# A two-layer hybrid trunk on one core: PSUM banks and norm weights of the SSD scan, row counts, sinks and rope of the sliding-window attention

## The chip, the core and the metric

The kernel runs on one core of a Trainium2 chip as one program. The core has TensorE (PE; its weight loads are shown as PEld), VectorE (DVE), ScalarE (ACT), GpSimd (POOL) and SyncE (SP, which here only issues DMAs). The metric is the device time of one execution in microseconds; lower is better. PSUM has eight banks of 512 f32 per partition, which is all that PE can write to.

## The reference

One token sequence of 1024 positions and width 1024 goes through two layers. Each layer projects the normalised input once and feeds three branches from it: sliding-window attention (SWA: 8 query heads, 2 key heads, rotary, one sink logit per head), forgetting attention (FoX) and a Mamba-2 SSD scan. Their outputs are concatenated and projected back; a memory cross-attention follows. Cut to the parts that the change touches:

```python
def rms_norm(x, w):
    return x * lax.rsqrt(jnp.mean(x * x, axis=-1, keepdims=True) + EPS) * w

def apply_rope(x, cos, sin):            # x1, x2: halves of the head
    return jnp.concatenate([x1 * c - x2 * s, x2 * c + x1 * s], axis=-1)

# sliding_window_attention, per block of 128 queries against 256 keys
scores = jnp.where(mask, q @ k.T * hd ** -0.5, NEG_INF)
m = jnp.maximum(jnp.max(scores, -1, keepdims=True), sink)
p = jnp.exp(scores - m)
probs = p / (jnp.sum(p, -1, keepdims=True) + jnp.exp(sink - m))

# ssd_chunked, per chunk of 128 positions and head h
y_diag = einsum('lsg,lsgh,sghp->lghp', c @ b.T, decay, xs)
y_off  = einsum('lgn,ghpn,lgh->lghp', c, carry, exp(acs))
yc = y_diag + y_off + d_skip * xs
yc = rms_norm(yc * silu(z), ssm_norm_w)
y  = concatenate([ya, yb, yc]) @ w_out
```

## The kernel before

Everything is f32 in effect. A large product is made of three fp32r matmuls: an operand is split into a high part (`hi`, an ACT copy, lines 75 to 79) and the remainder (`lo`, DVE or POOL, lines 81 to 85), and `mm3` (L110 to L113) adds high by high, low by high and high by low. Activations live transposed, features on the partitions, in two tiles `hhi` and `hlo` of 8 blocks of 128 features by 1024 positions.

**Order.** PE runs in the order in which the code emits its instructions. `mixer` weaves a main stream (FoX, then SWA, then the SSD scan) with a fill stream (projections, convolutions, gates, the output projection): the main stream yields what its step costs PE, or a point of a planned clock before which it does not go on, and `weave` puts fill work there (L297 to L325). The other engines' orders are made by a scheduler when the program is built. Each engine runs its list in order, so an instruction that waits holds up all that stand behind it. SP issues nearly all DMAs, in order.

**SWA.** There are 32 units per layer, 4 pairs of heads (t) by 8 query blocks (i), so 64 in all. `swa_project` (L740) makes Q of a pair by `roped` (L707): a projection into the PSUM tile `acc`, a scaled ACT copy to `qs`, four SBUF-to-SBUF DMAs that swap the halves, then cos on DVE (L719), sin on POOL (L720) and their sum (L721). A head's Q1 holds the high part twice, on partitions 0 to 63 and 64 to 127, K1 holds the high part of K above the low part of K, and Q2 holds Q's low part on 64 partitions. A unit's scores (`swa_scores`, L757) are two pairs of matmuls, one pair per head: Q1 by K1 over 128 rows (L769) and Q2 by K1's upper half over 64 rows (L770). Then DVE adds the mask and takes the maximum (L772), takes the smaller of the negated maximum and the negated sink (L778); L779 (DVE) and L780 (ACT) give exp(sink - m) in two columns, L782 (ACT) the exponentials with their row sums, L785 and L786 (DVE) the whole sum and its reciprocal, and POOL scales the tile Pt (L787). Three units later in the main stream `swa_turn` transposes Pt on PE (L798), ACT and DVE split it (ph, pl), and L830 multiplies by V. Pt rotates over four buffers under a tag that FoX uses too; the Q tiles rotate over three.

**SSD.** `ssd_scan` runs 16 units per layer, 8 chunks (c) by 2 groups (g). `before` of a unit is emitted one unit ahead: two matmuls `df` (L1069), C by B into the PSUM tile `pt` (`cb`, L1074), two activations that make the decay W (L1077, L1078), the mask (L1080), and W times `cb` (L1081). `after` makes the carried part in `yo` (L1095), the chunk state in `st` (L1105), the diagonal part in `yd` (L1124), adds them to Y (L1097, L1101, L1128), multiplies by the gate (L1129) and sums squares (L1130). `finish` of the chunk before follows each unit with g = 0: the root on POOL (L1142), the scaling of both halves Y on ACT (L1144), then for each half four transposes into `pt` (L1149) and, one block of 128 features after the other, `hi` (L79) and `lo` (L83) with a per-partition norm weight. `pt`, `yo`, `st` and `yd` are one PSUM bank each, `df` is two, and `acc` of the fill stream two.

## Time and profile before

| | us |
|---|---|
| median of 3 runs (2633.95 to 2640.07) | 2637.05 |
| the profiled execution, its own time | 2644.48 |
| its span, first to last instruction | 2642.7 |
| DVE busy in it | 1590.9 |
| ACT busy in it | 1219.2 |
| POOL busy in it | 1085.6 |

The spans of the stages of layer 0, by the first and last instructions of their lines: SWA from about 716 to 876 us, SSD from about 876 to 1110 us; of layer 1, SWA from about 1960 to 2107 us and SSD from about 2107 to 2350 us. The rest is the input norms, the projections, FoX and the cross-attention. In the rows of the profile `line engine op out<-in` comes first, then the count, the busy time, the mean of one in ns, and the idle time of the engine ahead of it with what ended that. A row of a timeline begins with its start and its duration in us; the durations of matmuls overlap, so it is the distance of two starts that tells what one costs. "L1149 <- DVE hlo L83" means that the instruction of line 1149 could start when that of line 83 was done.

### The profile page before, as it was taken

How to read it: one execution, taken by the hardware profiler on the slowest of the kernel's cores; microseconds unless marked ns; L12 is line 12 of the kernel's file. 1: busy time of each engine (PE TensorE's matmuls, PEld its weight loads, DVE VectorE, ACT ScalarE, POOL GpSimd, SP SyncE). 2: the span in 40 equal slices, each digit the busy share in tenths (PEclk: the TensorE clock that was granted, in tenths of full speed). 3: DMA queues.
4: the chain of work that ended last, by engine and by line, in shares of the span. 5: the costliest groups of instructions: out<-in, count | busy, mean ns of one | idle time of the engine just before them, and what ended most of it. 6: DMA issues, size and time to landing. Idle time of an engine off the chain costs nothing.

```text
span 2642.7 us, 39668 instructions
## 1 busy us (share of the span) xinstructions
PE 2527.8 (96%) x13900; PEld 2098.6 (79%) x13900; DVE 1590.9 (60%) x2940; ACT 1219.2 (46%) x2615; POOL 1085.6 (41%) x1081
## 2 busy tenths in 40 slices
PE   8799999999999988999999999999999998899997
PEld 7799988888777766778879988888877766577886
DVE  6823266666688666663464236666678867665445
ACT  5532254554466545534443135455455644443442
POOL 5642244444455544332252124344354555433233
PEclk9899999999999999999999999999999999999999
DMA  7673232222323745454364222222322465445333
GB/s 239 213 228 96 69 91 67 81 79 84 87 79 103 255 157 168 144 167 122 122 195 122 73 77 84 87 73 75 98 73 76 130 240 167 143 156 164 123 95 129
DMA packets 230363, 332.36 MB, mean 126 GB/s; under 512 B 24626, under 2 KB 107698, under 8 KB 230148
## 3 DMA queue, kind: packets, MB, share of 16 engines
q1 hardware_dynamic: 228292, 327.72, 39.9%
q8 instruction: 110, 1.80, 0.3%
q10 hardware_dynamic: 1872, 2.10, 0.2%
q14 instruction: 89, 0.73, 0.1%
HBM read 237.68 MB, written 86.81 MB: 123 GB/s over the span
## 4 chain that ended last, share of the span: by engine, by line
PE 76%; DVE 9%; DMA 5%; issue 3%; ACT 3%; POOL 2%; SPq 1%; DVEq 0%; ACTq 0%; POOLq 0%
PE acc L111 15%; PE acc L112 14%; PE acc L113 14%; PE tp L667 3%; PE tp L630 2%; PE big L372 2%; PE acc L372 2%; PE acc L374 2%; PE big L374 2%; PE acc L373 2%; PE big L373 2%; PE S L770 1%; PE big L598 1%; PE big L599 1%; PE tp L798 1%
## 5 line engine op out<-in xcount | busy, mean ns | idle before, releaser
L111 PE MATMUL acc<-hhi,whi 128*128 128x512 f32 (+1 forms) x1960 | 801.2, 409 | 2.4 <-DVE xt L1423 1.2
L113 PE MATMUL acc<-hlo,whi 128*128 128x512 f32 (+1 forms) x1960 | 771.9, 394 | 0.0
L112 PE MATMUL acc<-hhi,wlo 128*128 128x512 f32 (+1 forms) x1960 | 770.9, 393 | 0.0
L85 POOL TENSOR_TENSOR wlo<-wst,whi 128x512 fp32r<-128x512 f32 x279 | 376.8, 1351 | 402.3 <-ACT whi L77 337.1
L113 PEld LDWEIGHTS acc<-hlo,whi 128*128 128x128 f32 x1960 | 371.6, 190 | 82.0
L111 PEld LDWEIGHTS acc<-hhi,whi 128*128 128x128 f32 x1960 | 373.8, 191 | 69.6 <-issue 1.6
L112 PEld LDWEIGHTS acc<-hhi,wlo 128*128 128x128 f32 x1960 | 373.1, 190 | 58.0
L77 ACT CAST whi<-wst 128x512 fp32r<-128x512 f32 x420 | 259.5, 618 | 298.8 <-PE acc L113 196.3
L77 ACT CAST ph<-tp 128x512 fp32r<-128x512 f32 (+1 forms) x256 | 142.3, 556 | 180.6 <-PE tp L630 114.2
L85 DVE TENSOR_TENSOR pl<-tp,ph 128x512 fp32r<-128x512 f32 (+1 forms) x256 | 167.2, 653 | 80.1 <-ACT ph L77 78.0
L85 DVE TENSOR_TENSOR wlo<-wst,whi 128x512 fp32r<-128x512 f32 x141 | 114.1, 809 | 117.2 <-ACT whi L77 115.3
L609 POOL TENSOR_SCALAR Pt<-Pt,sm 128x128 f32<-128x128 f32 (+7 forms) x128 | 105.3, 823 | 189.6 <-DVE sm L608 187.5
L1011 DVE SCALAR_TENSOR_TENSOR ac<-u,cw,ac 128x512 f32<-128x512 f32 x144 | 129.1, 896 | 32.4 <-POOL ac L1006 31.0
L607 ACT ACTIVATE Pt<-big,sm 128x128 f32<-128x128 f32 (+7 forms) x128 | 95.0, 743 | 71.6 <-DVE sm L605 64.1
L85 POOL TENSOR_TENSOR tml<-tms,tmh 128x684 fp32r<-128x684 f32 (+3 forms) x40 | 67.8, 1714 | 134.3 <-ACT tmh L77 125.3
L604 DVE TENSOR_REDUCE sm<-big 128x1 f32<-128x128 f32 (+7 forms) x128 | 96.2, 752 | 23.4 <-PE big L601 21.9
L787 POOL TENSOR_TENSOR Pt<-Pt,mx 128x512 f32<-128x512 f32 x64 | 69.4, 1086 | 87.3 <-DVE mx L786 37.2
L372 PE MATMUL big<-tmh,hhi 128*128 128x342 f32 (+3 forms) x320 | 102.0, 319 | 1.0 <-DVE vt L85 1.0
L372 PE MATMUL acc<-tmh,hhi 128*128 128x342 f32 (+3 forms) x320 | 102.1, 319 | 0.0
L374 PE MATMUL acc<-tmh,hlo 128*128 128x342 f32 (+3 forms) x320 | 101.4, 317 | 0.0
L373 PE MATMUL big<-tml,hhi 128*128 128x342 f32 (+3 forms) x320 | 101.4, 317 | 0.0
L374 PE MATMUL big<-tmh,hlo 128*128 128x342 f32 (+3 forms) x320 | 101.4, 317 | 0.0
(338 smaller groups left out, 5242.1 us busy)
## 6 DMA issues: line engine op xcount, KB each, us to landing
wst<-in_w_fm_dram SPq DMA_DIRECT2D x132, 256.0 KB
wst<-in_w_out_dram SPq DMA_DIRECT2D x128, 256.0 KB
wst<-in_w_mq_dram SPq DMA_DIRECT2D x64, 256.0 KB
wst<-in_w_mo_dram SPq DMA_DIRECT2D x64, 256.0 KB
xt<-x_st SPq DMA_DIRECT2D x48, 256.0 KB
v_st<-vt SPq DMA_DIRECT2D x32, 320.0 KB
vs<-v_st SPq DMA_DIRECT2D x20, 512.0 KB
xs_st<-tr SPq DMA_DIRECT2D x40, 256.0 KB
```

Of the source, the lines that this page charges most:

```text
L77: self.nc.scalar.copy(out, in_)
L85: (eng or self.nc.vector).tensor_tensor(out=out, in0=in_, in1=f(hi), op=ALU.subtract)
L111: mm(ps, ahi, bhi, start=first, stop=False)
L112: mm(ps, alo, bhi, start=False, stop=False)
L113: mm(ps, ahi, blo, start=False, stop=last)
L372: mm(ps[:, :n], self.hhi[:, k, cs], hi[:, k, :n], start=k == 0, stop=False)
L373: mm(ps[:, :n], self.hhi[:, k, cs], lo[:, k, :n], start=False, stop=False)
L374: mm(ps[:, :n], self.hlo[:, k, cs], hi[:, k, :n], start=False, stop=k == KT - 1)
L604: nc.vector.tensor_reduce(out=sm[:, 0:1], in_=S[:, :n], axis=AX.X, op=ALU.max)
L607: nc.scalar.activation(Pt[:, :n], S[:, :n], AF.Exp, bias=sm[:, 1:2], scale=1.0, accum_out=sm[:, 2:3])
L609: nc.gpsimd.tensor_scalar(out=Pt[:, :n], in0=Pt[:, :n], scalar1=sm[:, 3:4], scalar2=1.0, op0=ALU.mult, op1=ALU.mult)
L1011: nc.vector.scalar_tensor_tensor(ac, u[:, 5 + j : 5 + j + HALF], w[:, t, j : j + 1], ac, ALU.mult, ALU.add)
```

## The change

Four edits:

1. **Banks of the SSD scan.** `pt`, `yo`, `st` and `yd` become one tag `s` with four rotating banks: each use takes the bank that was given out four uses ago.
2. **Norm weights at the gate.** `ssm_norm_w` is laid out by the host as a row of 1024 for each partition (512 KB to load per layer, 4 KB before). POOL multiplies it into Y right after the sum of squares, and `finish` splits four transposed blocks by one ACT copy and one DVE subtraction of 128x512, where four and four of 128x128 stood.
3. **SWA scores.** Q2 gets zeros on partitions 64 to 127 (two POOL fills of 64x1024 for each `swa_project`), and its matmul runs over 128 rows. The sinks are copied by POOL into column 256 of Pt, whose rows are 260 wide now; the exponentials run over 257 columns and their row sum holds the sink's share. The two small DVE additions and the small ACT exponential go.
4. **Rope.** The product with cos is taken by DVE straight from the PSUM tile, with the scale in it, and no more from `qs`.

```diff
@@ -716,7 +716,7 @@
             s = d + 32 if b % 2 == 0 else d - 32
             self.dma(qw[d : d + 32, :], qs[s : s + 32, :])
         qc = self.tile(pool, [P, HALF], F32, "G", 2)
-        nc.vector.tensor_tensor(out=qc, in0=qs, in1=self.cos[:, c], op=ALU.mult)
+        nc.vector.scalar_tensor_tensor(qc, ps, 1.0 if scale is None else scale, self.cos[:, c], ALU.mult, ALU.mult)
         nc.gpsimd.tensor_tensor(out=qw, in0=qw, in1=self.sin[:, c], op=ALU.mult)
         nc.vector.tensor_tensor(out=qc, in0=qc, in1=qw, op=ALU.add)
         return qc
@@ -738,11 +738,15 @@
                 self.lo(K1[g][64:128, c], src, K1[g][0:64, c])
 
     def swa_project(self, l, pool, t):
+        nc = self.nc
         Q1, Q2 = [
             [self.tile(pool, [P, T], F32R, nme, 3) for nme in ((n, n) if t % 2 == 0 else (n, o))]
             for n, o in (("q1", "k1"), ("q2", "k2"))
         ]
         self.state["swa", t] = Q1, Q2
+
+        for e in range(2):
+            nc.gpsimd.memset(f(Q2[e][64:128, :]), 0.0)
         wq = self.wload(self.a["w_fm"][l, T_QA + t])
         for half in range(2):
             c = slice(half * HALF, (half + 1) * HALF)
@@ -760,31 +764,31 @@
         Q1, Q2 = self.state["swa", t]
         K1 = self.state["swa"][0][t // 2]
         S = self.ps("S", 3)
-        Pt = self.tile(pool, [P, 2, 256], F32, "Pt", 4)
-        mx = self.tile(pool, [P, 6, 2], F32, "mx", 4)
+        Pt = self.tile(pool, [P, 2, 260], F32, "Pt", 4)
+        mx = self.tile(pool, [P, 4, 2], F32, "mx", 4)
+        h0 = 2 * t
+
+        nc.gpsimd.tensor_copy(Pt[:, :, 256], self.snk[:, h0 : h0 + 2])
         k0 = max(i - 1, 0) * P
         q = slice(i * P, (i + 1) * P)
         for e in range(2):
             o = S[:, e * 256 : (e + 1) * 256]
             mm(o, Q1[e][:, q], K1[:, k0 : k0 + 256], start=True, stop=False)
-            mm(o, Q2[e][0:64, q], K1[0:64, k0 : k0 + 256], start=False, stop=True)
+            mm(o, Q2[e][:, q], K1[:, k0 : k0 + 256], start=False, stop=True)
         for e in range(2):
             nc.vector.tensor_tensor_reduce(
-                out=Pt[:, e, :], in0=S[:, e * 256 : (e + 1) * 256], in1=self.band[:, min(i, 1), :], scale=1.0,
+                out=Pt[:, e, :256], in0=S[:, e * 256 : (e + 1) * 256], in1=self.band[:, min(i, 1), :], scale=1.0,
                 scalar=-3e38, op0=ALU.add, op1=ALU.max, accum_out=mx[:, 0, e : e + 1],
             )
-        h0 = 2 * t
 
         nc.vector.scalar_tensor_tensor(mx[:, 1], mx[:, 0], -1.0, self.nsk[:, h0 : h0 + 2], ALU.mult, ALU.min)
-        nc.vector.tensor_tensor(out=mx[:, 2], in0=self.snk[:, h0 : h0 + 2], in1=mx[:, 1], op=ALU.add)
-        nc.scalar.activation(mx[:, 3], mx[:, 2], AF.Exp)
         for e in range(2):
             nc.scalar.activation(
-                Pt[:, e, :], Pt[:, e, :], AF.Exp, bias=mx[:, 1, e : e + 1], scale=1.0, accum_out=mx[:, 4, e : e + 1]
+                Pt[:, e, :257], Pt[:, e, :257], AF.Exp, bias=mx[:, 1, e : e + 1], scale=1.0, accum_out=mx[:, 2, e : e + 1]
             )
-        nc.vector.tensor_tensor(out=mx[:, 5], in0=mx[:, 4], in1=mx[:, 3], op=ALU.add)
-        nc.vector.reciprocal(mx[:, 5], mx[:, 5])
-        nc.gpsimd.tensor_tensor(out=Pt, in0=Pt, in1=mx[:, 5, :, None].to_broadcast([P, 2, 256]), op=ALU.mult)
+        nc.vector.reciprocal(mx[:, 3], mx[:, 2])
+        o = Pt[:, :, :256]
+        nc.gpsimd.tensor_tensor(out=o, in0=o, in1=mx[:, 3, :, None].to_broadcast([P, 2, 256]), op=ALU.mult)
         return Pt
 
     def swa_turn(self, pool, Pt):
@@ -1070,7 +1074,7 @@
                     df[:, q * HALF : (q + 1) * HALF], SL[o : o + 32, cs], r[o : o + 32, :],
                     start=True, stop=True, tile_position=(o, 0),
                 )
-            cb = self.ps("pt")
+            cb = self.ps("s", 4)
             mm(cb[:, :P], bc[:, g, :], bc[:, 2 + g, :], start=True, stop=True)
             W = self.tile(sl, [P, 8, P], F32, "W", 2)
             W2 = W.rearrange("p h l -> p (h l)")
@@ -1091,7 +1095,7 @@
             hs = slice(8 * g, 8 * g + 8)
             xc, bc, _, ss, Ys = chunks[c]
             if c > 0:
-                yo = self.ps("yo")
+                yo = self.ps("s", 4)
                 mm(yo, bc[:, 2 + g, :], flat(carry[g]), start=True, stop=True)
                 t1 = self.tile(sl, B3, F32, "t1", 1)
                 nc.vector.tensor_tensor(
@@ -1101,7 +1105,7 @@
                 nc.gpsimd.tensor_tensor(out=Yg, in0=Yg, in1=t1, op=ALU.add)
                 yield 0.9
             if c < NB - 1:
-                st = self.ps("st")
+                st = self.ps("s", 4)
                 mm(st, xc[:, D + g * P : D + (g + 1) * P], flat(xts.pop((c, g))), start=True, stop=True)
                 new = carry[g] or self.tile(sl, B3, F32, f"ca{g}", 1)
                 if c == 0:
@@ -1118,7 +1122,7 @@
                 if c1 < NB - 1:
                     decayed(c1, g1, xd1)
             yield (at[c, g],)
-            yd = self.ps("yd")
+            yd = self.ps("s", 4)
             for h in range(8):
                 for m in (0, 64):
                     mm(
@@ -1128,6 +1132,7 @@
             nc.vector.tensor_tensor(out=Y, in0=yd, in1=Y, op=ALU.add)
             nc.vector.scalar_tensor_tensor(Y, Y, 0.5, zg, ALU.mult, ALU.mult)
             nc.scalar.activation(zg, Y, AF.Square, accum_out=ss[:, g : g + 1])
+            nc.gpsimd.tensor_tensor(out=Y, in0=Y, in1=nw[:, g * HALF : (g + 1) * HALF], op=ALU.mult)
             Ys.append(Y)
             yield 1.2
             at["Y", c] = self.clock
@@ -1144,15 +1149,13 @@
                 nc.scalar.activation(Ys[q], Ys[q], AF.Copy, bias=0.0, scale=ss[:, 3:4])
             yield (at["Y", c] + 9.0,)
             for q in range(2):
-                pt = self.ps("pt")
+                pt = self.ps("s", 4)
                 for k in range(4):
                     nc.tensor.transpose(pt[:, k * P : (k + 1) * P], Ys[q][:, k * P : (k + 1) * P], self.ident)
-
-                for k in range(4):
-                    m = 4 * q + k
-                    p, w = pt[:, k * P : (k + 1) * P], nw[:, m : m + 1]
-                    self.hi(self.hhi[:, m, cs], p, w)
-                    self.lo(self.hlo[:, m, cs], p, self.hhi[:, m, cs], w)
+                p3 = pt.rearrange("p (k d) -> p k d", d=P)
+                o = self.hhi[:, 4 * q : 4 * q + 4, cs]
+                self.hi(o, p3)
+                self.lo(self.hlo[:, 4 * q : 4 * q + 4, cs], p3, o)
                 yield 0.5
                 yield (self.clock + TURN,)
             self.ready.add(f"c{c}")
@@ -1160,7 +1163,7 @@
         units = [(c, g) for c in range(NB) for g in range(2)]
         at = {}
         load(0)
-        nw = self.load_w(sl, a["ssm_norm_w"][l], KT, "snw")
+        nw = self.load_w(sl, a["ssm_norm_w"][l], D, "snw")
         yield (self.clock + 14.0,)
         nxt = before(0, 0)
         decayed(0, 0, nxt[1])
@@ -1545,7 +1548,7 @@
     def col(w):
         return c(np.swapaxes(w.reshape(w.shape[:-1] + (w.shape[-1] // P, P)), -1, -2))
 
-    for n in ("norm_mix_w", "norm_xq_w", "norm_mem_w", "final_norm_w", "ssm_norm_w", "conv_b"):
+    for n in ("norm_mix_w", "norm_xq_w", "norm_mem_w", "final_norm_w", "conv_b"):
         r[n] = col(g[n])
     cw = g["conv_w"]
     r["conv_w"] = c(cw.reshape(L, 4, 12, P).transpose(0, 3, 2, 1))
@@ -1555,6 +1558,7 @@
 
     r["fdt_bias"] = rep(np.concatenate([g["b_forget"], g["dt_bias"]], -1))
     r["a_log"], r["d_skip"], r["sinks"] = rep(g["a_log"]), rep(g["d_skip"]), rep(g["swa_sinks"])
+    r["ssm_norm_w"] = rep(g["ssm_norm_w"])
 
     def fm(w):
         K, N = w.shape[1:]
```

PE has the same 11747 rows in the same order before and after, other tiles' names aside. The other four engines are ordered anew. Three places:

POOL at the end of FoX in layer 0, before. `Pt` with `sm` (L609) scales FoX probabilities, the last two rows of the last head having 896 and 1024 columns; `q` (L131) doubles Q's high part for SWA; `ph` and `pl` (L623, L624) are fills of FoX:

```order
L720 TENSOR_TENSOR stg_7321<-stg_7321,k_1339_7055 128x512
L623 MEMSET ph_7399 128x128
L624 MEMSET pl_7400 128x128
L609 TENSOR_SCALAR Pt_7359<-Pt_7359,sm_7356 128x896
L85 TENSOR_TENSOR wlo_7675<-wst_7672,whi_7674 128x512
L131 TENSOR_SCALAR q_1382_7245<-q_1382_7245 64x512
L131 TENSOR_SCALAR q_1383_7246<-q_1383_7246 64x512
L609 TENSOR_SCALAR Pt_7387<-Pt_7387,sm_7384 128x1024
```

POOL at the same place now, from the sin product ahead of it:

```order
L720 TENSOR_TENSOR stg_7323<-stg_7323,k_1339_7055 128x512
L749 MEMSET q_1424_7449 64x1024
L749 MEMSET k_1425_7450 64x1024
L623 MEMSET ph_7401 128x128
L624 MEMSET pl_7402 128x128
L609 TENSOR_SCALAR Pt_7361<-Pt_7361,sm_7358 128x896
L85 TENSOR_TENSOR wlo_7673<-wst_7670,whi_7672 128x512
L771 COPY Pt_7597<-snk_7059 128x2
L771 COPY Pt_7612<-snk_7059 128x2
L131 TENSOR_SCALAR q_1382_7245<-q_1382_7245 64x512
L131 TENSOR_SCALAR q_1383_7246<-q_1383_7246 64x512
L609 TENSOR_SCALAR Pt_7389<-Pt_7389,sm_7386 128x1024
```

Two fills of 64x1024 stand ahead of the FoX scaling of 896 columns, and two sink copies for SWA's first two units ahead of that of 1024 columns.

DVE in the SSD scan of layer 0, from the mask of one unit (L1080) to that of the next, in a unit that is followed by `finish`, before. `t` is the carried part (L1097), `ca` the carry (L1113), `xd` the next unit's input, `hlo` the low part that `finish` writes, `th` a sum of the fill stream:

```order
L1080 TENSOR_TENSOR pt_9983<-pt_9983,triu_555 128x128
L1097 TENSOR_TENSOR t_1935_9996<-yo_9994,E_561 128x512
L1113 TENSOR_TENSOR ca_1851_9588<-ca_1851_9588,st_9999 128x512
L1084 TENSOR_TENSOR xd_10118<-xc_9971,dt_560 128x512
L1081 TENSOR_TENSOR W_9985<-W_9985,pt_9983 128x1024
L1128 TENSOR_TENSOR Y_9903<-yd_10005,Y_9903 128x512
L85 TENSOR_TENSOR wlo_10175<-wst_10172,whi_10174 128x512
L1129 SCALAR_TENSOR_TENSOR Y_9903<-Y_9903,z_9889 128x512
L83 SCALAR_TENSOR_TENSOR hlo_72<-pt_10039,snw_9383,hhi_71 128x128
L1304 TENSOR_TENSOR th_9950<-acc_9964,th_9950 128x512
L83 SCALAR_TENSOR_TENSOR hlo_72<-pt_10039,snw_9383,hhi_71 128x128 x3
L83 SCALAR_TENSOR_TENSOR hlo_72<-pt_10081,snw_9383,hhi_71 128x128 x4
```

And now, with line numbers of the changed kernel (L1085 is W times `cb`, L1117 the carry, L1133 the gate; `s` is the rotating PSUM tile):

```order
L1084 TENSOR_TENSOR s_9919<-s_9919,triu_555 128x128
L1101 TENSOR_TENSOR t_1935_9932<-s_9930,E_561 128x512
L1085 TENSOR_TENSOR W_9921<-W_9921,s_9919 128x1024
L1117 TENSOR_TENSOR ca_1851_9532<-ca_1851_9532,s_9935 128x512
L1088 TENSOR_TENSOR xd_10043<-xc_9907,dt_560 128x512
L1132 TENSOR_TENSOR Y_9838<-s_9941,Y_9838 128x512
L85 TENSOR_TENSOR wlo_10101<-wst_10098,whi_10100 128x512
L1133 SCALAR_TENSOR_TENSOR Y_9838<-Y_9838,z_9824 128x512
L85 TENSOR_TENSOR hlo_72<-s_9976,hhi_71 128x4x128
L1307 TENSOR_TENSOR th_9886<-acc_9900,th_9886 128x512
L85 TENSOR_TENSOR hlo_72<-s_10012,hhi_71 128x4x128
```

W stands ahead of the carry and of `xd`, where it stood behind them, and there are two writes of `hlo` for each `finish` where there were eight.

POOL in the SSD scan of layer 0 where a chunk's root is taken, before (`sx` is the decayed input, `ss` the root, `Y` with `t` the sum with the carried part):

```order
L1054 TENSOR_TENSOR sx_10003<-xd_9990,dst_562 128x512
L1142 TENSOR_TENSOR ss_9569<-ss_9569,mhalf_124 128x1
L85 TENSOR_TENSOR wlo_10169<-wst_10166,whi_10168 128x512
L1110 TENSOR_TENSOR ca_1851_9588<-ca_1851_9588,cdec_563 128x512
L1101 TENSOR_TENSOR Y_9903<-Y_9903,t_1935_9996 128x512
L1054 TENSOR_TENSOR sx_10131<-xd_10118,dst_562 128x512
```

And now (L1135 is the product with the norm weights `snw`):

```order
L1058 TENSOR_TENSOR sx_9939<-xd_9926,dst_562 128x512
L85 TENSOR_TENSOR wlo_10095<-wst_10092,whi_10094 128x512
L1135 TENSOR_TENSOR Y_9727<-Y_9727,snw_9327 128x512
L1147 TENSOR_TENSOR ss_9513<-ss_9513,mhalf_124 128x1
L1114 TENSOR_TENSOR ca_1851_9532<-ca_1851_9532,cdec_563 128x512
L1105 TENSOR_TENSOR Y_9838<-Y_9838,t_1935_9932 128x512
L1058 TENSOR_TENSOR sx_10056<-xd_10043,dst_562 128x512
```

A low part of projection weights (`wlo`) and the product with the norm weights stand ahead of the root now; the carry's decay (`ca`) still follows it.

## The prediction

> **What bounds the kernel now.** I read the busy shares first, then a table by stage, then who PE waited for, and last the starts of single matmuls.
>
> ```profile
> PE 2527.8 (96%) x13900; PEld 2098.6 (79%) x13900; DVE 1590.9 (60%) x2940; ACT 1219.2 (46%) x2615; POOL 1085.6 (41%) x1081
> ```
>
> PE is busy for 96% of the span; no other engine is above 60%. So an edit off PE pays only where PE waits for it, and an edit on PE pays at once. The table by stage (start:end, length, then busy time of PE, PEld, DVE, ACT and POOL, granted clock, DMA share, GB/s) has the two SWA stages first and the two SSD stages below:
>
> ```profile
> 716.00:876.00 160.00, 157.60 (x760) 120.69 (x759) 128.50 (x373) 94.99 (x277) 79.57 (x72) 0.99 0.33 101
> 1960.00:2107.00 147.00, 145.62 (x703) 110.68 (x701) 122.32 (x357) 88.96 (x263) 72.47 (x66) 1.00 0.32 98
> 876.00:1110.00 234.00, 212.15 (x1295) 152.71 (x1294) 151.86 (x255) 114.50 (x215) 109.76 (x93) 0.96 0.55 177
> 2107.00:2350.00 243.00, 218.01 (x1322) 156.62 (x1323) 158.66 (x266) 118.93 (x227) 112.07 (x97) 0.96 0.52 171
> ```
>
> In SWA PE is full, at full clock. In SSD it idles 22 and 25 us, and its clock is 0.96. PE's waits over the whole span (total us, times, longest) say for whom:
>
> ```profile
> PE pt L1149 <- DVE hlo L83: 32.2, 16, 2.8
> ...
> PE pt L1149 <- DVE W L1081: 7.0, 6, 3.0
> ...
> PE pt L1074 <- DVE hlo L83: 6.2, 5, 1.8
> ...
> PE tp L798 <- POOL Pt L787: 2.8, 4, 1.1
> ```
>
> The three waits on the bank `pt` are 45.4 us, nearly all of that idle time. For SWA's softmax PE waited 2.8 us in all.
>
> **Edit 3, scores over 128 rows.** One unit's four matmuls on PE's timeline, with the two of the fill stream behind them:
>
> ```profile
> 787.59 0.28 PE L769 MATMUL S<-k,q 128*128 128x256 f32 x1
> 787.79 0.38 PE L770 MATMUL S<-k,q 64*128 64x256 f32 x1
> 788.11 0.38 PE L769 MATMUL S<-k,q 128*128 128x256 f32 x1
> 788.42 0.38 PE L770 MATMUL S<-k,q 64*128 64x256 f32 x1
> 788.73 0.50 PE L111 MATMUL acc<-hhi,whi 128*128 128x512 f32 x1
> 789.06 0.40 PE L112 MATMUL acc<-hhi,wlo 128*128 128x512 f32 x1
> ```
>
> From the first start to L111's are 1.14 us, for 4 x 256 columns; L111 itself is followed 0.33 later. Matmuls of 256 columns elsewhere, first of FoX with 128 and 68 rows, then SWA's product with V:
>
> ```profile
> 321.82 0.28 PE L598 MATMUL big<-k,q 128*128 128x256 f32 x1
> 321.93 0.28 PE L599 MATMUL big<-k,q 68*128 68x256 f32 x1
> 322.05 0.23 PE L601 MATMUL big<-nmaskb,identb 128*128 128x128 bf16 x1
> ```
>
> ```profile
> 781.56 0.40 PE L830 MATMUL tp<-ph,vs 128*128 128x256 f32 x2
> 781.79 0.39 PE L830 MATMUL tp<-pl,vs 128*128 128x256 f32 x2
> 782.02 0.39 PE L111 MATMUL acc<-hhi,whi 128*128 128x512 f32 x1
> 782.26 0.40 PE L112 MATMUL acc<-hhi,wlo 128*128 128x512 f32 x1
> ```
>
> There each costs 0.12 us, new weights for each one included, and L112 follows L111 by 0.24. FoX's 68 rows next to 128 cost nothing; 64 rows next to 128 cost about 0.2 at each change. So a unit falls from 1.14 to 4 x 0.12 = 0.48, and L111 behind it by 0.09: 0.75 us. The matmuls of L770 give the count:
>
> ```profile
> L770 PE MATMUL S<-k,q x96: 379/382/383, 717.1 to 2106.3; 64*128 64x256 f32 x96
> ...
> L770 PE MATMUL S<-k,k x32: 381/381/382, 749.6 to 2106.9; 64*128 64x256 f32 x32
> ```
>
> 128 are 64 units: **48 us** off a full PE; 42 if L111's share stays. The Trainium skill ("TensorE: Matmul & The Clock Gate", section "Why this matters for your kernels") says that a single matmul of 32 contraction rows takes the same time as one of 128; by that alone the padding is worth nothing and this term would be 0. The rows of 1.14 and 0.12 speak against reading it so where the two row counts alternate.
>
> What the edit adds: 16 POOL fills of 64x1024 and 64 copies of two columns. The profile has neither; of the nearest rows the first is a fill of 128 columns:
>
> ```profile
> L1101 POOL TENSOR_TENSOR Y<-Y,t 128x512 f32<-128x512 f32 x28 | 35.9, 1284 | 8.4 <-DVE t L1097 8.4
> ...
> L623 POOL MEMSET ph<- 128x128 f32 x64 | 13.1, 204 | 157.3 <-PE acc L373 102.7 <-PE tp L667 54.1
> ```
>
> A fill is between 0.2 us (no growth) and 8 x 0.204 = 1.6; I take 1.0. It matters where PE already waits for POOL, at the end of FoX:
>
> ```profile
> 702.85 1.43 POOL L609 TENSOR_SCALAR Pt<-Pt,sm 128x1024 f32<-128x1024 f32 x1
> ```
>
> ```profile
> 704.33 0.55 PE L630 MATMUL tp<-ident,Pt 128*128 128x128 f32 x3 [1.22 <-POOL Pt L609]
> ```
>
> Two fills and two copies now stand ahead of that scaling, and behind it are PE's transposes: 0.4 to 3.6 us per layer come straight onto PE; I take 2, **4 us** for both. The copies must also wait until PE has transposed the tile that used their buffer; in POOL's order they stand some two units ahead of their own scaling, so the scaling behind them is still early. The other fills hide: POOL is half idle in SWA, and softmax is ready ahead of PE in nearly all units. That cover failing is rival A.
>
> What it removes is off PE's path: two DVE additions and an ACT exponential per unit.
>
> ```profile
> L779 DVE TENSOR_TENSOR mx<-snk,mx 128x2 f32<-128x2 f32 x64 | 18.2, 286 | 0.9
> ...
> L785 DVE TENSOR_TENSOR mx<-mx 128x2 f32<-128x2 f32 x64 | 18.1, 283 | 7.1 <-ACT mx L780 6.9
> ...
> L719 DVE TENSOR_TENSOR G<-stg,k 128x512 f32<-128x512 f32 x20 | 16.8, 842 | 2.6 <-ACT stg L79 2.4
> ```
>
> It keeps DVE as it was: 128.5 of 160 us now, 110 of 136 then, 0.80 and 0.81. The softmax gets 0.6 us shorter, PE asks for it about 1.5 us sooner (two groups of scores). The first units of each layer, where the 2.8 us of waits are, lose 0 to 3 us per layer; I take 1, **2 us** in all.
>
> **Edit 4, rope**, trades one DVE operation for another of the same size (L719, 20 in all). It holds the bank `acc` until DVE comes to it rather than ACT, while PE fills the other `acc` bank for 24 matmuls (24 x 0.23 = 5.5 us). Between -1 and +3 us; I take 0.
>
> **Edit 1, the banks.** Two transposes of one `finish`, and the next unit's `yd`:
>
> ```profile
> 924.79 1.11 PE L1149 MATMUL pt<-ident,Y 128*128 128x128 f32 x4 [2.98 <-DVE W L1081]
> ...
> 931.81 0.66 PE L1149 MATMUL pt<-ident,Y 128*128 128x128 f32 x4 [2.15 <-DVE hlo L83]
> ...
> 937.81 1.15 PE L1124 MATMUL yd<-xd,W 128*64 128x64 f32 x32
> ```
>
> The second group waits for the split of the first, and the next `cb` for that of the second. In the rotation `cb, yo, st, yd, pt, pt` the second group takes the bank of `yo` and the next `cb` that of `st`, both read long before: 32.2 + 6.2 = **38.4 us** go. What waits for the splits now are `st` and `yd` of the next unit; `yd` comes 6.0 us after the second group. The first group still takes the bank of the same step's `cb`, which W times `cb` reads. In DVE's new order that product stands ahead of the carry, except at each layer's first `finish`, where the 2.98 was: I leave 6.0 of the 7.0 and count **1 us**.
>
> The clock: 0.04 of 234 + 243 us are 19 us. They lie in eleven windows of 3.4 us at half clock, the first and the last of them here:
>
> ```profile
> 924.50:927.90 3.40, 3.11 (x10) 2.63 (x11) 2.56 (x6) 1.34 (x4) 1.62 (x2) 0.50 0.49 151
> ...
> 2303.40:2306.90 3.50, 3.50 (x6) 1.33 (x6) 2.21 (x3) 0.67 (x1) 1.19 (x2) 0.51 0.25 77
> ```
>
> Each costs 1.7 us of PE's work. The first begins inside the wait of 2.98; the SWA stages, where PE hardly waits, run at 0.99 and 1.00. Two should stay with the wait that stays; of 9 x 1.7 = 15 I take **13 us**, the bounds being 0 and 19. The Trainium skill (same page and section) puts the drop at idle gaps above about 3 us. By that rule these waits, 3.0 us at most, do not cause it and the 13 us stay lost; the row above speaks against it, and rival C prices it.
>
> **Edit 2, the norm weights.** The split goes from four ping-pongs of ACT and DVE to one:
>
> ```profile
> L79 ACT ACTIVATE hhi<-pt,snw 128x128 fp32r<-128x128 f32 x128 | 46.6, 364 | 64.4 <-PE pt L1149 35.4 <-DVE hlo L83 29.0
> ...
> L83 DVE SCALAR_TENSOR_TENSOR hlo<-pt,snw,hhi 128x128 fp32r<-128x128 f32 x128 | 44.6, 348 | 57.0 <-ACT hhi L79 57.0
> ...
> L85 DVE TENSOR_TENSOR hlo<-tp,hhi 128x512 fp32r<-128x512 f32 x32 | 22.1, 691 | 21.7 <-ACT hhi L77 21.6
> ```
>
> DVE's part falls from 44.6 to 32 x 0.69 = 22 us; no longer on PE's path, it pays nothing more. The product adds 32 x 1.28 = 41 us to POOL (the row of L1101), which goes from 110 of 234 to 130 of some 210 us. It delays the root and with it the first transposes, which PE's waits never name: 0 to 32 x 1.28 / 2 = 20 us, I take 1. The load of 512 KB per layer takes 3 us at the stage's 175 GB/s on SP's queue, ahead of the first gate and of weights: 0 to 6, I take 2.
>
> **Sum.** SWA 48 - 4 - 2 = 42; SSD 38.4 + 1 + 13 - 1 - 2 = 49; 91 us. The profiled execution took 2644.48 us (span 2642.7 and 1.8 around it), so 2553.5; it lies 7.4 above the median of 2637.05, so 2546 for the median.
>
> **Rivals.** A: SWA's softmax becomes the bound. DVE's share of 0.8 and POOL's new work speak for it, the 2.8 us of waits against; half of the 48 lost, 67 us: 2570. B: SSD's waits move, to W or to `yd`; half of the 49 lost: 2570. C: the clock stays at 0.96 in SSD: 78 us, 2559. D, the change doesn't do what it says: the 0.2 us at each change are not of the row count; 0 for 48: 43 us, 2594. E, slower: DVE runs the second `hlo` only behind the next unit's W and `xd`. Then `yd`, which takes that bank, waits at each of 14 finishes; with 8 us each and a half-clock window, 14 x 9.7 = 136 us replace the 49 won, with 42 from SWA: 2682. It decides from 6.5 us per finish, that is if `hlo` ends over 12 us after its transposes. DVE's rows, which have `hlo` ahead of the next mask, speak against it.
>
> **Chances.** Forecast 0.60 (its own range 2524 to 2562), C 0.10, A 0.12, B 0.11, D 0.05, E 0.02. The lower end takes all of 48 and of 45.4 + 19, the upper end A or B with 12 us on top: 2524 to 2582. The measurement tells about 0.2% from no change. Faster 0.96, within it 0.02, slower 0.02.
>
> **What would show it.** Four score matmuls within 0.5 us; no wait of the transposes on `hlo`; granted clock 0.98 or more in SSD; SWA stages of some 137 and 126 us, SSD of some 209 and 218. A long row of PE waiting for the scaling of Pt would show A, for W or in `yd` B. The forecast falls most easily if several of these waits, each small, grow together once PE no longer hides them.

## The result and the profile after

| | before | after |
|---|---|---|
| median of 4 runs (of before one more than ahead of the prediction), us | 2638.07 (2633.95 to 2640.07) | 2540.49 (2536.86 to 2551.32) |
| profiled execution, us | 2644.48 | 2551.32 |

The ratio of after to before is 0.9639, with a 95% interval of 0.9607 to 0.9671: 95 us by the ratio, 97.6 between the medians, where 91 were forecast. The profiled execution of after is its slowest of four, 10.8 us above the median.

The busy shares of after, as at the head of the prediction:

```profile
PE 2466.7 (97%) x13900; PEld 2081.7 (82%) x13900; DVE 1545.4 (61%) x2716; ACT 1189.0 (47%) x2455; POOL 1166.9 (46%) x1193
```

PE is still what everything waits for, and still issues 13900 instructions. They stand in the same order as before, so one can cut both executions at the same instruction. I took SWA from the first score matmul to the scan's first `df` matmul, SSD from there to the start of the last transpose of `finish`, and as all else what remains between the starts of PE's first and last matmuls. Each stage's length is split in three: PE's waits (sum of its idle times), the loss to the clock (half of the time of each half-clock window), and the rest, PE's own work at full clock. Both layers added, us:

| stage | before: length = work + waits + clock | after: length = work + waits + clock | change |
|---|---|---|---|
| SWA | 353.0 = 346.0 + 5.3 + 1.7 | 325.0 = 298.3 + 18.2 + 8.5 | -28.0 |
| SSD | 412.8 = 348.7 + 45.3 + 18.8 | 346.8 = 345.2 + 1.5 + 0.0 | -66.0 |
| all else | 1864.0 | 1864.4 | +0.4 |

These stages are longer than the prediction's windows, which were cut at round times and left out their ends; its lengths of 137, 126, 209 and 218 us are therefore not held against the table. So SWA gained less than the 42 forecast, and SSD more than the 49. The table by stage of after, columns as in the prediction, SWA first:

```profile
713.00:860.00 147.00, 138.87 (x775) 118.11 (x774) 114.57 (x310) 91.67 (x246) 91.03 (x104) 0.98 0.37 113
1911.00:2062.00 151.00, 141.14 (x780) 119.63 (x779) 115.67 (x311) 92.63 (x248) 91.13 (x104) 0.97 0.36 110
858.00:1062.00 204.00, 202.95 (x1300) 149.16 (x1299) 148.88 (x209) 103.38 (x167) 134.04 (x109) 1.00 0.65 211
2060.00:2256.00 196.00, 195.31 (x1267) 142.84 (x1266) 144.81 (x201) 100.95 (x163) 132.14 (x108) 1.00 0.63 208
```

The two stages have changed places: PE is now full in SSD, at a clock of 1.00, and idles 8 and 10 us in SWA, at 0.98 and 0.97. Whom PE waited for (total us, times, longest), from the same view as before:

```profile
...
PE acc L111 <- DVE th L510: 5.4, 2, 2.8
PE tp L802 <- POOL Pt L791: 5.1, 7, 1.1
...
PE tp L630 <- POOL Pt L609: 4.4, 2, 2.2
PE tp L802 <- DVE ys L542: 4.0, 6, 1.0
PE tp L802 <- DVE pl L85: 2.4, 2, 1.2
...
PE s L1128 <- DVE W L1085: 1.2, 2, 0.8
...
PE s L1154 <- ACT Y L1149: 0.2, 1, 0.2
```

Of the 45.4 us of waits on the bank `pt` nothing is left: the transposes (now L1154) wait 0.2 us in all, neither for `hlo` nor for W. The waits of SWA's transposes (L802) on Pt and `ys` and of the projection (L111) on the gate's product are new or have grown. Inside the SWA stages PE waited 5.4 us for the gate's product, 5.1 for Pt, 4.0 for `ys` and 3.5 for `pl` (before: 1.0, 2.8, 0 and 1.3); but for Pt, DVE writes all of these. The score matmuls of one unit, with two of the fill stream behind:

```profile
768.46 0.27 PE L776 MATMUL S<-k,q 128*128 128x256 f32 x1
768.58 0.28 PE L777 MATMUL S<-k,q 128*128 128x256 f32 x1
768.69 0.28 PE L776 MATMUL S<-k,k 128*128 128x256 f32 x1
768.81 0.28 PE L777 MATMUL S<-k,k 128*128 128x256 f32 x1
768.93 0.40 PE L111 MATMUL acc<-hhi,whi 128*128 128x512 f32 x1
769.16 0.40 PE L112 MATMUL acc<-hhi,wlo 128*128 128x512 f32 x1
```

From the first start to that of L111 are 0.47 us, where they were 1.14, and L112 follows after 0.23, where it was 0.33.

The operations that the trace of before did not show, and the split of `finish` (the mean in ns stands behind the bar's first number):

```profile
L1135 POOL TENSOR_TENSOR Y<-Y,snw 128x512 f32<-128x512 f32 x32 | 44.0, 1375 | 29.0 <-ACT z L1134 26.2 <-DMA wst<-in_w_out_dram 2.9
...
L85 DVE TENSOR_TENSOR hlo<-s,hhi 128x512 fp32r<-128x512 f32 x32 | 21.8, 682 | 10.8 <-ACT hhi L77 10.8
...
L771 POOL COPY Pt<-snk 128x2 f32<-128x2 f32 x64 | 18.8, 299 | 17.4 <-PE tp L802 13.3 <-PE tp L630 3.6
L77 ACT CAST hhi<-s 128x512 fp32r<-128x512 f32 x32 | 18.7, 586 | 18.3 <-PE s L1154 18.3
...
L749 POOL MEMSET q<- 64x1024 f32 x12 | 11.3, 952 | 11.3 <-PE big L601 11.0
```

A fill took 0.95 us (1.0 was taken), a copy 0.30, a product 1.38 (1.28 was taken). The split of four transposes lasts 0.59 + 0.68 = 1.27 us now; before it was a chain of ACT and DVE in turn, 4 x (0.364 + 0.348) = 2.85 us by the prediction's rows.

The two largest new waits stand at the end of SWA, 2.54 us in layer 0 and 2.85 in layer 1. That of layer 0, from the timeline of all engines (a bracket gives the engine's idle time before the instruction, and what ended it):

```profile
839.27 2.52 SPq L72 DMA_DIRECT2D SR<-sr_st  x1
...
841.89 0.38 SPq L72 DMA_DIRECT2D hlo<-y_st  x1
...
845.82 0.62 ACT L77 CAST hhi<-hlo 128x512 fp32r<-128x512 f32 x1 [2.17 <-DMA hlo<-y_st]
846.34 0.59 ACT L509 ACTIVATE th<-acc 128x512 f32<-128x512 f32 x1
...
846.96 0.69 DVE L510 SCALAR_TENSOR_TENSOR th<-th,acc 128x512 f32<-128x512 f32 x1 [2.85 <-ACT th L509]
...
847.70 0.50 PE L111 MATMUL acc<-hhi,whi 128*128 128x512 f32 x1 [2.54 <-DVE th L510]
```

Read it upwards: PE needs the bank that the gate's tanh and product (L509, L510) read; the tanh stands on ACT behind the cast of an early `y`; that `y` lands late, because SP issued its load behind those that the code for the scan places there (the last, SR, alone took SP 2.52 us).

### The profile page after: what moved, and what is told of

It is laid out like the page before. It is cut to its first block, busy times and chain, and to the rows that moved or that the text cites. A ratio compares the mean times of both kernels' runs of the same rounds, so it can differ in the third digit from the quotient of the medians.

```text
span 2549.3 us, 39348 instructions
## 1 busy us (share of the span) xinstructions
PE 2466.7 (97%) x13900; PEld 2081.7 (82%) x13900; DVE 1545.4 (61%) x2716; ACT 1189.0 (47%) x2455; POOL 1166.9 (46%) x1193
## 4 chain that ended last, share of the span: by engine, by line
PE 78%; DVE 7%; DMA 5%; issue 3%; ACT 3%; POOL 3%; SPq 1%; DVEq 0%; POOLq 0%; ACTq 0%
PE acc L111 16%; PE acc L112 15%; PE acc L113 15%; PE tp L667 3%; PE tp L630 2%; PE acc L372 2%; PE big L372 2%; PE acc L374 2%; PE big L374 2%; PE acc L373 2%; PE big L373 2%; SPq L72 1%; PE big L598 1%; PE big L599 1%; PE s L1128 1%
## 5 line engine op out<-in xcount | busy, mean ns | idle before, releaser
L111 PE MATMUL acc<-hhi,whi 128*128 128x512 f32 (+1 forms) x1960 | 796.8, 407 | 6.8 <-DVE th L510 5.4
L112 PE MATMUL acc<-hhi,wlo 128*128 128x512 f32 (+1 forms) x1960 | 771.6, 394 | 0.0
L111 PEld LDWEIGHTS acc<-hhi,whi 128*128 128x128 f32 x1960 | 374.2, 191 | 67.3 <-DVE th L510 5.8
L112 PEld LDWEIGHTS acc<-hhi,wlo 128*128 128x128 f32 x1960 | 373.8, 191 | 57.7
L85 DVE TENSOR_TENSOR wlo<-wst,whi 128x512 fp32r<-128x512 f32 x141 | 128.4, 910 | 118.0 <-ACT whi L77 117.2
L609 POOL TENSOR_SCALAR Pt<-Pt,sm 128x128 f32<-128x128 f32 (+7 forms) x128 | 105.8, 827 | 182.6 <-DVE sm L608 180.0
L373 PE MATMUL acc<-tml,hhi 128*128 128x342 f32 (+3 forms) x320 | 101.4, 317 | 0.0
```

The source lines that it names most:

```text
L85: (eng or self.nc.vector).tensor_tensor(out=out, in0=in_, in1=f(hi), op=ALU.subtract)
L111: mm(ps, ahi, bhi, start=first, stop=False)
L112: mm(ps, alo, bhi, start=False, stop=False)
L373: mm(ps[:, :n], self.hhi[:, k, cs], lo[:, k, :n], start=False, stop=False)
L609: nc.gpsimd.tensor_scalar(out=Pt[:, :n], in0=Pt[:, :n], scalar1=sm[:, 3:4], scalar2=1.0, op0=ALU.mult, op1=ALU.mult)
```

## The experiments

All are variants of the changed kernel, but for "128 rows alone", a variant of the kernel before. Except where the planned time or the ratio of the planner was altered, PE's instructions are in the same order as in both kernels, so the stages can be cut as above. The results together (stages in us, both layers, from one profiled execution each; `w` waits, `c` clock). The ratios are to runs of the kernel before on the same chip, whose medians were 2637.4 to 2639.2 us:

| kernel | SWA (w, c) | SSD (w, c) | median, us | ratio to before, 95% |
|---|---|---|---|---|
| before | 353.0 (5.3, 1.7) | 412.8 (45.3, 18.8) | 2638.07 | 1 |
| after | 325.0 (18.2, 8.5) | 346.8 (1.5, 0.0) | 2540.49 | 0.9639, 0.9607 to 0.9671 |
| scores on 64 rows | 345.8 (0.7, 0.0) | 346.7 (1.4, 0.0) | 2562.58 | 0.9709, 0.9689 to 0.9728 |
| sinks as before | 338.2 (31.4, 6.8) | 346.2 (1.0, 0.0) | 2556.49 | 0.9687, 0.9664 to 0.9711 |
| before, with 128 rows alone | 336.6 (29.4, 6.8) | 413.3 (47.5, 17.1) | 2628.81 | 0.9950, 0.9930 to 0.9971 |
| banks apart | 318.9 (17.3, 1.7) | 359.8 (9.3, 5.1) | 2546.24 | 0.9643, 0.9621 to 0.9664 |
| split as before | 322.9 (18.9, 5.1) | 348.6 (2.9, 0.0) | 2540.66 | 0.9631, 0.9609 to 0.9653 |
| rope as before | 321.6 (18.8, 3.4) | 347.2 (1.9, 0.0) | 2543.07 | 0.9636, 0.9614 to 0.9658 |
| late loads | 320.2 (16.1, 5.1) | 346.0 (0.8, 0.0) | 2538.30 | 0.9614, 0.9592 to 0.9636 |
| late loads, softmax first | 322.7 (19.3, 3.4) | 346.7 (1.4, 0.0) | 2536.82 | 0.9617, 0.9599 to 0.9634 |

Four of these have the code of SWA's units as in the changed kernel (after, banks apart, split and rope as before): 318.9 to 325.0, so one profile tells SWA to some 6 us. For SSD the six kernels with both of its edits lie within 346.0 and 347.2. What lies outside the two stages is less steady, 1863 to 1880 us of the span in these ten, so a few us between medians tell little of a stage.

**Scores on 64 rows.**

```diff
-        for e in range(2):
-            nc.gpsimd.memset(f(Q2[e][64:128, :]), 0.0)
...
-            mm(o, Q2[e][:, q], K1[:, k0 : k0 + 256], start=False, stop=True)
+            mm(o, Q2[e][0:64, q], K1[0:64, k0 : k0 + 256], start=False, stop=True)
```

> The changed kernel, with Q2's score matmul on 64 rows again and without the POOL fills; all else as changed. Row theory (the alternation of 128 and 64 rows is what cost PE time): a unit's four score matmuls take 1.14 us again in place of 0.47, the two SWA stages' PE content grows by about 48 us (from 149 to 173 per layer), their waits and half-clock windows shrink back from some 20 us towards 5, so the whole time grows by 28 to 48 us, to about 2570 to 2588. Rival (SWA's gain came from the shorter softmax chain, not from the rows): the time stays within 8 us of the changed kernel's 2540.5.

It came 22 us above after. The work of PE in the SWA stages is 345.2 us again, 46.9 more than after, and the matmuls show it:

```profile
769.92 0.27 PE L774 MATMUL S<-k,q 128*128 128x256 f32 x1
770.13 0.38 PE L775 MATMUL S<-k,q 64*128 64x256 f32 x1
770.44 0.39 PE L774 MATMUL S<-k,k 128*128 128x256 f32 x1
770.75 0.38 PE L775 MATMUL S<-k,k 64*128 64x256 f32 x1
771.06 0.50 PE L111 MATMUL acc<-hhi,whi 128*128 128x512 f32 x1
```

1.14 us again: the row count is the cause, and the rival falls. The waits and clock losses of SWA vanish (0.7 and 0.0), so the longer matmuls had covered the work of the other engines. The whole time rose by less than the 28 expected at least.

**Sinks as before** (two DVE additions and ACT's exponential per unit, no copies; after otherwise).

```diff
-        nc.gpsimd.tensor_copy(Pt[:, :, 256], self.snk[:, h0 : h0 + 2])
...
+        nc.vector.tensor_tensor(out=mx[:, 2], in0=self.snk[:, h0 : h0 + 2], in1=mx[:, 1], op=ALU.add)
+        nc.scalar.activation(mx[:, 3], mx[:, 2], AF.Exp)
...
+        nc.vector.tensor_tensor(out=mx[:, 5], in0=mx[:, 4], in1=mx[:, 3], op=ALU.add)
```

> The changed kernel with the sinks handled as before (two DVE additions and an ACT exponential per unit, no copies of two columns on POOL); scores over 128 rows and the fills stay. Theory (SWA gives back because PE asks for the softmax sooner than its chain delivers, and the chain was shortened by 0.6 us): the waits of the SWA stages grow from 8 to 10 us per layer by 1 to 6 us, the whole time by 2 to 12 us. Rival (the copies on POOL, which wait for PE and stand ahead of the scalings, make those waits): the waits on the scaling of Pt (5 to 6 us over the kernel) go and the time falls by 3 us or more.

16 us slower at the medians, more than expected; the two intervals overlap a little (0.9664 to 0.9671), but the SWA stages, at 338.2 us, lie 13 to 19 above the four profiles with the new sinks. The waits in its trace:

```profile
PE tp L803 <- POOL Pt L792: 13.8, 7, 3.9
PE tp L803 <- DVE ys L542: 10.9, 6, 3.1
```

against 5.1 and 4.0 in after. The copies on POOL are not what PE waits for: without them, but with the longer softmax, PE's waits in SWA are 31.4 us in place of 18.2. An edit to which the prediction gave no time of its own is worth some 13 to 16 us, once PE asks sooner.

**128 rows alone**, on the kernel before, with the fills and nothing else.

```diff
+        for e in range(2):
+            self.nc.gpsimd.memset(f(Q2[e][64:128, :]), 0.0)
...
-            mm(o, Q2[e][0:64, q], K1[0:64, k0 : k0 + 256], start=False, stop=True)
+            mm(o, Q2[e][:, q], K1[:, k0 : k0 + 256], start=False, stop=True)
```

> The kernel before with one edit alone: Q2's score matmul over 128 rows, with the POOL fills of its upper half. Theory: PE content of the two SWA stages falls by 48 us (173 to 149 per layer), the waits and the half-clock windows there rise by some 20 us as in the changed kernel, whatever the other edits are, and the SSD stages stay at 205 and 208 us: 20 to 30 us below the kernel before, at 2608 to 2618. Rival (the give-back comes from the sinks' copies and the other edits): some 40 us below, at 2598 or less.

```profile
PE pt L1151 <- DVE hlo L83: 32.4, 16, 2.8
PE tp L800 <- POOL Pt L789: 12.0, 6, 3.7
...
PE tp L800 <- DVE ys L542: 10.3, 6, 3.0
```

It gained 10 us only (9.3 to 2638.07), less than either theory said. SWA's work falls by 45.6 us, its waits rise by 24.1 and the clock's loss by 5.1: 16.4 us are left in the stage. The SSD waits are unaltered (32.4 against 32.2 on `hlo`), so the 128 rows do not reach into that stage; and with SSD's edits undone one at a time, below, SWA stays at 318.9 and 322.9.

How the softmax and PE stand to each other can be worked out from the traces. For each of the 64 units I took the time from the start of its last score matmul to the end of POOL's scaling of its Pt (the chain), and to the point at which PE had finished what stands ahead of the unit's transposes (PE asks). The third column is the chain's first part, up to the start of DVE's mask and maximum, with the time in it that DVE was busy with other instructions; us:

| kernel | chain, mean | until the mask (DVE busy) | PE asks, median | PE asks, least |
|---|---|---|---|---|
| before | 7.66 | 1.19 (0.98) | 10.99 | 9.54 |
| scores on 64 rows (short chain) | 6.57 | 0.95 (0.72) | 10.96 | 8.57 |
| before, 128 rows alone (long chain) | 8.88 | 2.47 (2.44) | 9.50 | 7.73 |
| after | 7.46 | 1.95 (1.77) | 9.27 | 7.74 |

The 128 rows take 1.5 to 1.7 us from the time that a unit has, and lengthen the chain by 0.9 to 1.2 us. That growth is all in the first part (1.0 and 1.3 us): the mask stands in DVE's list behind `pl`, `ys` and work for the projections and gates, and DVE is still at that. Two things push that way, and the runs do not part them: the same DVE work comes in less time (DVE is busy for 74.5% of the SWA stages in after, 71.2% with 64 rows), and the last score matmul starts 0.35 us after the first in place of 0.83, so the chain's clock starts sooner. The sinks' edit shortens the chain by 1.1 to 1.4 us. In after PE asks before the chain has ended in seven of the 64 units, the first, second and fourth of each layer and one more, whose chains are 8.7 to 11.1 us.

**Banks apart**: `cb` and the transposes share one bank again, `yo`, `st` and `yd` have one each; the norm weights stay at the gate.

```diff
-            cb = self.ps("s", 4)
+            cb = self.ps("pt")
-                yo = self.ps("s", 4)
+                yo = self.ps("yo")
...
-                pt = self.ps("s", 4)
+                pt = self.ps("pt")
```

> The changed kernel, with the scan's PSUM tiles in banks of their own again (cb and the transposes in one, yo, st and yd in one each) and the norm weights still multiplied in at the gate. Bank theory: waits of the transposes and of cb for the split come back, since the next transposes again need the bank that the split still reads; with a split of one pair in place of four a wait is about 1 us in place of 2.15, so 12 to 30 us of waits over the 22 places and some half-clock windows of 1.7 us each: the whole time grows by 12 to 45 us, to 2553 to 2585, all of it in the two SSD stages (173 us each in the changed kernel). Rival (the shorter split made SSD's gain, the banks little): less than 10 us.

```profile
PE pt L1154 <- DVE W L1085: 6.1, 4, 3.4
...
PE pt L1078 <- DVE W L1085: 3.2, 2, 2.1
```

SSD is 13.0 us longer (7.8 waits, 5.1 clock), which is the lower end of the bank theory's range. The median of the whole time is 5.8 us longer with overlapping intervals, which is the rival's range; the profiled execution is even 4.7 us shorter than that of after, as SWA and all else came out shorter in it. The stage decides here, and it bears out the bank theory in size only. The waits are not those that the theory named: none is on `hlo`. With the short split, the work that the planner puts between two groups (L1160 sets 2.2 of its clock) covers it: the split ends 1.7 to 2.8 us after the first group's last transpose, and PE asks for the second group after 2.9 us at the least. In the kernel before it ended after 4.1 to 6.7 us, and PE asked after 3.0 to 4.6. What comes back are the waits on W, which the prediction had meant to stay.

**Split as before**: four banks, but the norm weights in the split again (eight operations of 128x128) and no product on POOL.

```diff
-            nc.gpsimd.tensor_tensor(out=Y, in0=Y, in1=nw[:, g * HALF : (g + 1) * HALF], op=ALU.mult)
...
+                for k in range(4):
+                    m = 4 * q + k
+                    p, w = pt[:, k * P : (k + 1) * P], nw[:, m : m + 1]
+                    self.hi(self.hhi[:, m, cs], p, w)
+                    self.lo(self.hlo[:, m, cs], p, self.hhi[:, m, cs], w)
```

> The changed kernel with four rotating banks, but with the norm weights applied in the split of the transposes as before (eight operations of 128x128 on ACT and DVE for each group) and no product on POOL at the gate. Bank theory: PE still finds another bank free, the two SSD stages stay near 173 us each, the whole time within 10 us of 2540.5. Rival (the long split comes back in another wait): st, yd or the next transposes wait for the bank whose split now lasts 2 us longer, 1 to 2 us at each of 16 finishes and half-clock windows with it, so 20 to 50 us more, to 2560 to 2590.

Its two longest waits in SSD:

```profile
PE s L1128 <- DVE t L1101: 2.2, 2, 1.3
...
PE s L1109 <- DVE hlo L83: 0.4, 1, 0.4
```

SSD is 1.9 us longer than after, the whole time the same. So of SSD's 66.0 us the banks alone bring 64.1 and the short split alone 53.0: each of the two removes the waits on `hlo`. The short split adds next to nothing to the banks; the banks add 13.0 us to the short split, by the waits on W.

**Rope as before.**

```diff
-        nc.vector.scalar_tensor_tensor(qc, ps, 1.0 if scale is None else scale, self.cos[:, c], ALU.mult, ALU.mult)
+        nc.vector.tensor_tensor(out=qc, in0=qs, in1=self.cos[:, c], op=ALU.mult)
```

> The changed kernel with the rope's cosine product taken from the scaled copy again, not from PSUM. Theory (one DVE operation for another of the same size, the PSUM bank read long before PE needs it): within 3 us of the changed kernel's 2540.5. Rival (holding the bank until DVE comes to it costs PE a wait in the projections): 3 to 8 us faster than the changed kernel, with fewer waits of the projections in the parts before the SWA stages.

2543.07 against 2540.49, intervals nearly the same: no effect that can be told, as forecast.

**Late loads**: the loads that stood ahead of the early `y` are issued some units later (after unit `len(units) - 2`), so SP issues that `y` first.

```diff
+            if u == len(units) - 2:
+                self.early_loads()
...
```

> The changed kernel, with four loads that stand at the start of the SSD preparation (D skip, the S rows, the first B and C rows) issued some units later, so that SP issues the last early load of y ahead of them. Theory (that load comes late, ACT's cast of it stands ahead of the gate's tanh, and PE waits for the gate's product): the wait of 2.5 and 2.8 us before the matmuls of line 111 at the end of each SWA stage goes, and with it half-clock windows of 3.4 and 6.8 us (1.7 and 3.4 us of PE's work): 5 to 10 us less in the SWA stages, so 2531 to 2536. Rival (the cast is late for another reason, or the wait is of the gate itself): the wait stays, time within 2 us of 2540.5. Second rival: the loads that come later make SSD's first step wait, and the time grows by 3 us or more.

```profile
PE acc L111 <- DVE th L510: 2.9, 2, 1.9
```

The wait fell from 5.4 to 2.9 us (1.0 and 1.9 in the two layers), so the late load made half of it; what is left of it was not tested. The median is 2.2 us lower, and the intervals overlap: neither theory's time is shown.

Three tries, each on top of the late loads, to win back more. **More planned time** from a unit's scores to its transposes:

```diff
-                at[u] = self.clock + 7.0
+                at[u] = self.clock + 9.0
```

> The late loads of the run before, and the planned time from a SWA unit's scores to its transposes raised from 7 to 9, so that the planner puts two more groups of the fill stream between them where it can. Theory (what is left of SWA's give-back are the units where the softmax chain is later than PE): the two first waits of each layer (1.1 to 1.7 us each) shrink and no new one appears: 4 to 8 us less than with the late loads alone, so 2530 to 2534. Rival (the fill stream is short and the units crowd later): the waits move to later units, time within 3 us of 2538.

```profile
PE tp L834 <- DVE pl L85: 15.9, 14, 2.1
...
PE tp L802 <- POOL Pt L791: 3.7, 2, 2.0
```

2544.55 us, ratio 0.9642 (0.9627 to 0.9656): the waits moved from the transposes to the product with V (L834), for which PE asks 3.0 us after the unit's last transpose at the median, where it was 5.0 with the late loads alone. **More fill work per unit**:

```diff
-            self.ratio = 1.9
+            self.ratio = 2.3
```

> The late loads, and the planner's ratio of fill work to SWA's own work raised from 1.9 to 2.3, so that more projection matmuls stand between a unit's scores and its transposes all through the stage (the 48 us that the scores no longer take had been cover for the softmax chain). Theory (SWA's give-back is a matter of pace: PE asks for a unit's softmax 1.7 us sooner than before): the waits of the two SWA stages fall from 8 to 10 us per layer to some 3 to 5, the whole time by 5 to 12 us against the late loads alone, so 2526 to 2533. Rival (other work on DVE and ACT comes closer together just as well, or the fill stream is used up before the last units): the waits move or stay, within 3 us of 2538 or slower.

```profile
PE acc L111 <- ACT hhi L77: 8.9, 4, 4.2
...
PE acc L111 <- DVE th L510: 7.1, 2, 3.6
PE s L1134 <- DVE W L1091: 7.0, 2, 3.5
```

2567.84 us, ratio 0.9725 (0.9705 to 0.9746), 29.5 slower than the late loads. SWA's scores are spread over more time, from the first to the last 145.8 and 143.3 us in the two layers, where they were 131.7 and 129.7, and PE now waits for casts (`hhi`, 8.9 us) that are not ready. **Softmax first**, a unit's softmax (L778 to L791) at the priority that the casts of its probabilities already have:

```diff
+        with self.tc.high_priority(100):
```

> The late loads, and the softmax instructions of a SWA unit (mask and maximum, exponentials, reciprocal, scaling) put ahead of the other work in the orders of DVE, ACT and POOL. Theory (from the scores to the scaled Pt a unit takes 7.5 us at the median, of which its own instructions are about 4 us, the rest is standing behind other work): the chain falls to 5 to 6.5 us, the waits on Pt and ys in the SWA stages mostly go, 5 to 12 us less than with the late loads alone, so 2526 to 2533. Rival (what is put behind it, the casts of the projections and of the probabilities, is late instead): waits of the projections or of PV grow by as much, within 3 us of 2538 or slower.

```profile
PE tp L803 <- DVE ys L542: 5.7, 5, 2.1
PE tp L803 <- POOL Pt L792: 4.4, 3, 1.7
```

2536.82 us. The mean chain is 7.60 us, not shorter (7.46 with the late loads alone), and the waits are as long. The priority did not bring the mask forward: it starts 2.11 us after the last score matmul (1.87 with the late loads alone), and for 2.04 of them DVE is busy with other instructions. So the theory was not put to the test; how much the chain would gain by an earlier mask stays open. The two lowest medians, this and the late loads, have intervals that overlap after's: no version is shown to beat it.

## Why the prediction came out as it did

The forecast of -91 us was close to the -97.6 measured, and in part by luck: SWA gave some 15 us less than forecast and SSD 17 more. The matmuls and the waits that the change takes away were named rightly.

- **Scores, -48.** The mechanism and the price were right: 47.8 us of PE's work went, and 46.9 came back with the 64 rows. Read as a rule for alternating matmuls, the Trainium skill's sentence that few rows cost the same as 128 ("TensorE: Matmul & The Clock Gate", "Why this matters for your kernels") would have made this 0; the traces do not agree.
- **What SWA gives back.** The step "the first units of each layer [...] lose 0 to 3 us per layer; I take 1, 2 us in all" was mis-sized, and it is the step that failed in SWA: waits grew by 12.9 us and the clock's loss by 6.8, 19.7 of 47.8 in this profile (12.0 to 19.7 in the four with these units). The prediction set PE asking 1.5 us sooner (1.5 to 1.7 measured), against a chain 0.6 us shorter, and took the difference to be covered. It left out that DVE comes later to the mask (the chain grows by 0.9 to 1.2 us), and counted only DVE's two additions, while the sinks' edit shortened the chain by 1.1 to 1.4. That edit, said to be off PE's path, was worth some 13 to 16 us. Rival A, which had half of the 48 lost, was near in size, but the softmax is only part of it: of the 12.9 us of new waits 2.3 are for Pt, the others for `ys` (4.0), the gate's product (4.4) and `pl` (2.2), which DVE hands to PE.
- **End of FoX, +4.** Right in kind: PE's wait for the last scaling rose from 2.7 to 4.4 us, and is 2.6 in the kernel without fills, 4.9 in the one with fills and no copies; so +1.7 for both layers, the fills' alone.
- **The waits on `hlo`, -38.4.** They went. But the prediction gave them to the banks alone; the runs show that either edit removes them.
- **"The first group still takes the bank of the same step's `cb`"** is wrong, and so is "the bank that was given out four uses ago" in the description of the change. The prediction let the banks rotate in order of use. The built program does not: at each layer's first `finish`, after `cb` in bank 7, `yo` in 6, `st` in 5 and `yd` in 4, the two groups of transposes are given 6 and 5. The first group never gets `cb`'s bank (it is `yo`'s in 12 of 16); the second does in 10 of 16, and PE asks for it 2.9 us after the first. This would fit a pool that hands out the bank that comes free first; its rule was not looked into. No transposes wait for W: all 7.0 us went, the 2.98 at each layer's first `finish` with them, and with a bank shared with `cb` waits on W come back (banks apart).
- **The clock, -13.** The whole upper bound of 19 came, because the two waits that were to stay did not. Rival C (the clock stays at 0.96) is out.
- **Product and load, +3.** The product cost POOL 44.0 us (41 forecast) and the cover held: SSD's waits are 1.5 us in all. Nothing of the load is seen.
- **Rope, 0.** As measured.
- **Rivals B, D and E** did not happen: PE's waits for W at `yd` (L1128) are 1.2 us in all, those on `hlo` in the scan none. E's price was also added up otherwise than said: if 136 us replaced the 49 won, with 42 from SWA, the time would be 2731; 2682 keeps the 49.

Added up from the profiled executions: SWA -28 where -42 was said (with +1.7 of FoX's end outside the stage), SSD -66 where -49 was said, with all else the sum is -93.6, beside 93.2 between the times of the two executions. PE's work in SSD also fell by 3.5 us, which was not followed up.

## What to carry to other kernels

When a matmul on a full PE gets shorter, set for each dependent chain its length against the time at which PE now asks for it, unit by unit with the tails, and let the chain grow: here DVE came to it 1.0 to 1.3 us later, and handed PE its other results later too. Two edits that remove the same wait must not be credited twice: test each alone. Where a pool hands out buffers, look up which one it gave; a rotation in order of use is an assumption.

## What was not expected of the hardware

The prediction tied the half-clock windows to the waits of SSD. One in SWA of after followed a much shorter wait. Below are that window, the 3.6 us ahead of it, and the matmul at its start:

```profile
725.60:729.10 3.50, 3.44 (x10) 2.90 (x11) 2.71 (x8) 1.02 (x2) 2.50 (x5) 0.51 0.59 169
722.00:725.60 3.60, 1.88 (x12) 1.21 (x10) 1.65 (x6) 3.54 (x12) 3.28 (x4) 1.00 0.40 91
```

```profile
725.66 1.11 PE L802 MATMUL tp<-ident,Pt 128*128 128x128 f32 x4 [1.11 <-POOL Pt L791]
```

The wait was 1.11 us, with one of 0.67 us 2.2 us ahead of it; PE was busy for 1.88 of the 3.60 us before the clock fell to 0.51. The Trainium skill (same page and section) puts the drop at idle gaps above about 3 us; this trace does not agree. Where no wait is over 0.9 us, in SSD of after, there is no such window.

A single wait is not what counts in these traces. Within each of the twelve, all half-clock windows start on a fixed grid of 3.41 us: the two at 725.7 and 848.6 us of after, for example, are 36 steps apart. I took PE's busy share in every step of the grid that ran at full clock, over all twelve traces but for their first and last few steps. Of the 126 steps with less than 45%, all were followed by a half-clock window; of the 8502 with 55% or more, 5; in between, 24 of 76. So what goes with the clock of the next step is how much PE idles in a whole step: here 1.11 and 0.67 us together, 52% of it. A longer wait that is shared by two steps can pass without a window, as one of 3.7 us did in the run "128 rows alone" (up to 1965.8 us; 54% of each step idle, in the range where both happen).
